# The first norm of a two-layer diffusion backbone: squares by blocks, feature sums as one-column products, and an opening order written out by hand

## Chip, cores and metric

The kernel runs on one core of one Trainium2 chip. The metric is the device time of one execution in microseconds (us). The core has five engines with a queue each: TensorE (PE in the profile; its weight loads are shown apart as PEld), VectorE (DVE), ScalarE (ACT), GpSimd (POOL) and SyncE (SP), which here issues all DMAs. An instruction waits at the head of its engine's queue until its semaphores are there, and what stands behind it on that engine waits too.

## The reference, cut to what matters

```python
def rms_norm(x, g):
    y = x * lax.rsqrt(jnp.mean(x * x, axis=-1, keepdims=True) + EPS)
    return y * g

def adaln(cond, w, b):                       # cond: c for the latent, c_ctx for the context
    return (jax.nn.silu(cond) @ w + b).reshape(cond.shape[0], N_MOD, 1, D_MODEL)

def half_ffn(h, shift, scale, gate, g, w1, w3, w2):
    n = modulate(rms_norm(h, g), shift, scale)       # n * (1 + scale) + shift
    return h + 0.5 * gate * ((jax.nn.silu(n @ w1) * (n @ w3)) @ w2)

for l in range(DEPTH):                       # 2 layers
    m, mc = adaln(c, ada_w[l], ada_b[l]), adaln(c_ctx[None], ada_w[l], ada_b[l])
    h  = half_ffn(h,  m[:, 0],  m[:, 1],  m[:, 2],  norm_g[l, 0], ...)
    hc = half_ffn(hc, mc[:, 0], mc[:, 1], mc[:, 2], norm_g[l, 0], ...)
    ...                                      # four token mixers, merge, second half FFN
```

There are 256 latent and 256 context tokens with 1024 features, all in float32. The part that matters is the very first: the norm of h over its features, the modulation 0 (shift) and 1 (scale) from a product with `ada_w`, and the first columns of `w1` and `w3`.

## The kernel before

Activations lie with features on partitions: `h` is 128 x 8 x 512, that is 8 feature blocks b of 128, and 512 columns, 256 latent and 256 context tokens. Every large product is made in three float32r products (`mm3`, lines 197 to 199): the operands are cut into a high and a low part, `hi`/`lo` for weights (`cut`, lines 182 and 183: a copy on ACT, a difference on DVE) and `nh`/`nl` for the normalised h (lines 409 and 416). A weight column is 1024 x 128, 512 KB, loaded by `raw` (line 171) into a ring of three buffers, from which `cut` makes its split; the load that is to take a buffer over waits for the DVE half of the split before it.

`start` (line 214) opens the program. It loads the small parameters, h in two halves (latent, context), the constants (`ones` and `ident`), and then, in between each other, five groups of the shift and scale columns of `ada_w` (`adaraw0` to `adaraw4`, for the feature blocks 0, 1, 2 to 3, 4 to 5, 6 to 7; 1, 1, 2, 2 and 2 MB, each with a buffer of its own) and four weight columns, called `p1_0`, `p3_0`, `p1_1`, `p3_1`. The norm squares each half of h on ACT in one instruction (line 247), sums it over the 8 blocks on DVE (`ssum`, line 248), turns that by four transposes on PE (line 368), so that a DVE reduce can sum over the 128 partitions (line 370), and then makes the reciprocal root, spreads it over 128 columns (`n_w`, line 374) and turns it back on PE (`turn`, line 379; the rstd rows).

The loop over the groups then makes the modulation of a group (32 small plain float32 products, line 257), transposes it on DVE (`adat`, line 263), normalises its blocks (`nt`, `nh`, `nl`; lines 402, 409, 416) and multiplies the blocks that are ready with the columns that are split. Each column needs 8 blocks x 3 products, so there are 96 early products. Columns for later stages (`raw20`, `raw21`, ... by the order of loading) are loaded and split in `high_priority`, which lets a scheduler move them ahead of other work on their engines. Behind the early products the program goes on with the column of `raw20`.

The lines that carry the norm:

```python
for cols in (LAT, CTX):
    q = pool.tile([128, DB, T], F32, tag="q", name=f"q{cols.start}", bufs=1)
    nc.scalar.activation(out=q, in_=self.h[:, :, cols], func=AF.Square)
    nc.vector.tensor_reduce(out=ssum[:, cols], in_=q.rearrange("p b t -> p t b"), axis=AX.X, op=ALU.add)
turn = self.rstd(ssum, 512, D, "n00")
```

Of the kernel before, what the change touches and what calls it, by code (L numbers as in the profile page):

```python
# [10 lines left out]
F32 = mybir.dt.float32  # L11
F32R = mybir.dt.float32r
AF = mybir.ActivationFunctionType
ALU = mybir.AluOpType
# [104 lines left out]
class Build:  # L119
# [94 lines left out]
    def start(self, pool):  # L214
# [3 lines left out]
        nc.sync.dma_start(out=self.small, in_=d["small"])  # L218
        for cols in (LAT, CTX):
            nc.sync.dma_start(out=self.h[:, :, cols], in_=d["h0"][:, :, cols])  # L220
        nc.sync.dma_start(out=self.const, in_=d["const"][:, 0:EARLY])
        raw, columns, banks = [], [], {}
        first = [(f"p{n}_{i}", f"ffn_w{n}", i) for i in (0, 1) for n in (1, 3)]
        groups = [range(a, b) for a, b in ((0, 1), (1, 2), (2, 4), (4, 6), (6, 8))]
        loaded = (1, 2, 3, 4, 4)
        for gi, group in enumerate(groups):
# [7 lines left out]
            with self.tc.high_priority():  # L234
                nc.sync.dma_start(out=raw[gi].rearrange("p k f -> p (k f)").rearrange("p (c f) -> p c f", f=1024),
                                  in_=d["wst"][i:i + 2 * n].rearrange("c p f -> p c f"))
            for key, name, i in first[len(columns):loaded[gi]]:
                columns.append(self.raw(self.columns(name, (0, 0), np.arange(128 * i, 128 * i + 128))))
# [5 lines left out]
        ssum = self.held("ssum")  # L244
        for cols in (LAT, CTX):
            q = pool.tile([128, DB, T], F32, tag="q", name=f"q{cols.start}", bufs=1)
            nc.scalar.activation(out=q, in_=self.h[:, :, cols], func=AF.Square)
            nc.vector.tensor_reduce(out=ssum[:, cols], in_=q.rearrange("p b t -> p t b"), axis=AX.X, op=ALU.add)
        turn = self.rstd(ssum, 512, D, "n00")
        done, ready, split = [0] * len(first), 0, 0  # L250
        for gi, group in enumerate(groups + [()]):
            n = len(group)
            if n:
                ps = self.aux(f"ada0{gi}")
                for k in range(DB):
                    for g in range(4):
                        nc.tensor.matmul(ps[32 * g:32 * g + 32, 0:64 * n], self.st[:, k, :],
                                         raw[gi][:, k, 64 * n * g:64 * n * (g + 1)], start=k == 0, stop=k == DB - 1)
                if gi == 0:
                    r = turn()  # L260
                    parts = [self.norm_parts(0, 0, s, r[:, c]) for s, c in enumerate((LAT, CTX))]
                t = self.temp(f"adat0{gi}", 64 * n)
                nc.vector.transpose(out=t, in_=ps[:, 0:64 * n])
                for m in (0, 1):
                    self.modulated(0, m, t.rearrange("p (b m r) -> p m b r", m=2, r=32)[:, m, :, 0:2],
                                   slice(group[0], group[-1] + 1))
                for b in group:
                    for part in zip(*parts):
                        for f in part:
                            f(b)  # L270
            for i in range(split):
                if i not in banks:
                    banks[i] = (self.acc, self.pair)[i % 2](first[i][0])
                for k in range(done[i], ready):
                    self.mm3(banks[i], columns[i][k], self.n(k, ALL), k == 0, k == DB - 1)
                done[i] = ready
            ready += n
            for i in range(split, loaded[gi] if n else 0):
                columns[i] = self.cut(columns[i], pool=pool, bufs=4)
            split = loaded[gi] if n else split  # L280
        self.early = {first[i][0]: banks[i] for i in banks}
        c = pool.tile([128, 2, D], F32, tag="q", name="condrow", bufs=1)
# [76 lines left out]
    def rstd(self, x, n, count, name, heads=1):  # L359
# [7 lines left out]
        for i in range(nt):  # L367
            nc.tensor.transpose(ps[:, 128 * i:128 * i + 128], x[:, 128 * i:128 * i + 128], self.cst("ident"))
        r = self.tmp.tile([128, 8], F32, tag="rs", name=f"{name}_s", bufs=2)
        nc.vector.tensor_reduce(out=r[:, 0:m], in_=ps[:, 0:n].rearrange("p (m f) -> p m f", m=m), axis=AX.X, op=ALU.add)  # L370
# [6 lines left out]
        def turn(ps=ps):  # L377
            for i in range(nt):
                nc.tensor.transpose(ps[:, 128 * i:128 * i + 128], w[:, 128 * i:128 * i + 128], self.cst("ident"))
# [257 lines left out]
    def mixing(self, l, closing):  # L637
# [5 lines left out]
        with self.tc.tile_pool(name=f"mix{l}", bufs=2) as mp:  # L643
# [5 lines left out]
            nc.sync.dma_start(out=self.late, in_=self.d["const"][:, EARLY:])  # L649
# [517 lines left out]
```

## Time and profile before

| what | value |
|---|---|
| median of 3 runs | 2267.54 us (2266.43 to 2267.88) |
| the profiled execution | 2266.95 us, span 2265.2 us |
| mean granted TensorE clock in it | 0.997 |
| PE busy | 2216.1 us, 98% of the span |
| DVE busy, ACT busy | 1479.9 us (65%), 964.6 us (43%) |
| PE busy in the first 20 us | 1.90 us |
| moved by DMA | 322.81 MB, mean 143 GB/s |

The median of the runs is the time; the profile is of one execution, whose span begins with its first and ends with its last instruction. A line of the timeline has start and length in us, engine, source line, operation, what is written from what, shapes and count; brackets hold the idle time before it and what ended it. An SPq line is a DMA's issue; the DMA view gives the time from the issue to the landing.

### The profile page before, as it was taken

To read this page: it belongs to the slowest core of one execution; us is meant where nothing else is said; L and a number is where in the kernel's file an instruction comes from. 1 tells how busy PE (TensorE), PEld (TensorE's weight loads), DVE (VectorE), ACT (ScalarE), POOL (GpSimd) and SP (SyncE) were. 2 spreads that over 40 slices of the span, in tenths; PEclk is the share of its full clock that TensorE was granted. 3 is DMA by queue.
4 is the path that set the end of the run, shared out by engine and by line. 5 is a ranking of instruction groups with operands and counts; after the bars stand their busy time and mean duration, and the time that the engine had idled before them with its cause. 6 is when DMAs were issued, how large, how long until landed. Compare 5 with 4: busy or idle time off the path is not lost.

```text
span 2265.2 us, 32288 instructions
## 1 busy us (share of the span) xinstructions
PE 2216.1 (98%) x12822; PEld 1915.5 (85%) x12822; DVE 1479.9 (65%) x2432; ACT 964.6 (43%) x1513; POOL 117.7 (5%) x124
## 2 busy tenths in 40 slices
PE   6999999999999999999999999999999999999998
PEld 4888889888888788888888898888889898998998
DVE  6788874794778645556565545665537889775554
ACT  4323223455557633342222232223224777754443
POOL 0000000000000112110000010000001000121000
PEclk9999999999999999999999999999999999999999
DMA  8566663311222232334544424454534333454553
GB/s 323 184 202 202 207 214 117 119 66 65 75 75 75 75 103 93 112 112 153 163 161 156 155 82 145 158 167 149 165 115 170 122 121 122 139 181 164 180 184 131
DMA packets 92742, 322.81 MB, mean 143 GB/s; under 512 B 9904, under 2 KB 15280, under 8 KB 91952
## 3 DMA queue, kind: packets, MB, share of 16 engines
q1 hardware_dynamic: 92592, 320.76, 42.4%
q8 instruction: 100, 1.64, 0.3%
q14 instruction: 50, 0.41, 0.1%
HBM read 315.48 MB, written 5.24 MB: 142 GB/s over the span
## 4 chain that ended last, share of the span: by engine, by line
PE 87%; DVE 9%; ACT 3%; issue 1%; DMA 0%; POOL 0%; DVEq 0%; SPq 0%; ACTq 0%; POOLq 0%
PE p L198 12%; PE p L199 12%; PE p L197 12%; PE pr L199 7%; PE pr L198 6%; PE pr L197 6%; PE g L197 3%; PE g L198 3%; PE g L199 3%; DVE cv L699 2%; DVE lo L183 2%; PE b L197 2%; PE b L198 2%; PE b L199 2%; PE ao L889 1%
## 5 line engine op out<-in xcount | busy, mean ns | idle before, releaser
L182 ACT ACTIVATE hi<-raw 128x1024 fp32r<-128x1024 f32 x430 | 454.6, 1058 | 885.7 <-issue 250.1
L183 DVE TENSOR_TENSOR lo<-raw,hi 128x1024 fp32r<-128x1024 f32 x422 | 526.2, 1248 | 293.1 <-ACT hi L182 286.9
L197 PE MATMUL p<-nh,hi 128*128 128x512 f32 (+1 forms) x1456 | 521.7, 358 | 2.4 <-ACT nh L409 1.3
L199 PE MATMUL p<-nh,lo 128*128 128x512 f32 (+1 forms) x1456 | 520.9, 358 | 2.5 <-DVE lo L183 2.5
L198 PE MATMUL p<-nl,hi 128*128 128x512 f32 (+1 forms) x1456 | 521.2, 358 | 1.2 <-DVE nl L416 1.1
L325 DVE SCALAR_TENSOR_TENSOR prods<-raw,cond 128x1024 f32<-128x1024 f32 x240 | 289.1, 1222 | 191.5 <-DMA raw<-wst 188.6
L197 PEld LDWEIGHTS p<-nh,hi 128*128 128x128 f32 x1456 | 276.6, 190 | 43.8 <-ACT nh L409 2.2
L199 PEld LDWEIGHTS p<-nh,lo 128*128 128x128 f32 x1456 | 276.6, 190 | 42.9 <-DVE lo L183 3.7
L198 PEld LDWEIGHTS p<-nl,hi 128*128 128x128 f32 x1456 | 276.6, 190 | 41.5 <-DVE nl L416 2.1
L199 PE MATMUL pr<-gh,lo 128*128 128x512 f32 (+1 forms) x656 | 231.4, 353 | 0.0
L198 PE MATMUL pr<-gl,hi 128*128 128x512 f32 (+1 forms) x656 | 229.4, 350 | 0.0
L197 PE MATMUL pr<-gh,hi 128*128 128x512 f32 (+1 forms) x656 | 228.4, 348 | 0.0
L197 PE MATMUL g<-nh,hi 128*128 128x512 f32 (+1 forms) x512 | 174.9, 342 | 0.0
L199 PE MATMUL g<-nh,lo 128*128 128x512 f32 (+1 forms) x512 | 173.4, 339 | 0.0
L198 PE MATMUL g<-nl,hi 128*128 128x512 f32 (+1 forms) x512 | 172.6, 337 | 0.0
L699 DVE SCALAR_TENSOR_TENSOR cv<-yp,cw,cv 128x512 f32<-128x512 f32 (+1 forms) x240 | 148.7, 620 | 4.8
L198 PEld LDWEIGHTS pr<-gl,hi 128*128 128x128 f32 x656 | 123.2, 188 | 19.4
L197 PEld LDWEIGHTS pr<-gh,hi 128*128 128x128 f32 x656 | 123.6, 188 | 18.0
L199 PEld LDWEIGHTS pr<-gh,lo 128*128 128x128 f32 x656 | 123.1, 188 | 17.0
L197 PEld LDWEIGHTS g<-nh,hi 128*128 128x128 f32 x512 | 97.0, 189 | 10.5 <-issue 0.6
L199 PEld LDWEIGHTS g<-nh,lo 128*128 128x128 f32 x512 | 97.0, 189 | 10.4 <-issue 0.2
L198 PEld LDWEIGHTS g<-nl,hi 128*128 128x128 f32 x512 | 97.0, 190 | 9.9 <-issue 0.2
(427 smaller groups left out, 3415.7 us busy)
## 6 DMA issues: line engine op xcount, KB each, us to landing
raw<-wst SPq DMA_DIRECT2D x556, 512.0 KB, 3.4
adaraw<-wst SPq DMA_DIRECT2D x3, 2048.0 KB, 17.1
adaraw<-wst SPq DMA_DIRECT2D x8, 512.0 KB, 7.4
cond<-cond SPq DMA_DIRECT2D x3, 1024.0 KB, 4.8
h<-h SPq DMA_DIRECT2D x2, 1024.0 KB, 7.9
adaraw<-wst SPq DMA_DIRECT2D x2, 1024.0 KB, 10.6
parked<-h SPq DMA_DIRECT2D x8, 256.0 KB, 3.9
h<-parked SPq DMA_DIRECT2D x8, 256.0 KB, 3.1
```

Source lines behind the costliest of these rows:

```text
L182: self.nc.scalar.activation(out=hv, in_=r, func=AF.Copy)
L183: getattr(self.nc, low).tensor_tensor(out=lv, in0=r, in1=hv.bitcast(F32), op=ALU.subtract)
L197: mm(out, w[0], x[0], start=start, stop=False)
L198: mm(out, w[0], x[1], start=False, stop=False)
L199: mm(out, w[1], x[0], start=False, stop=stop)
L325: nc.vector.scalar_tensor_tensor(out=products[:, s], in0=r, scalar=1.0, in1=cond[:, s], op0=ALU.mult, op1=ALU.mult, accum_out=self.mod[l][ ...
L699: nc.vector.scalar_tensor_tensor(out=o, in0=x, scalar=wk, in1=o, op0=ALU.mult, op1=ALU.add)
L889: nc.tensor.matmul(o[64 * a:64 * a + 64, 0:128], va[:, k0 + k, 64 * a:64 * a + 64], at[j, qt][a][:, 128 * k:128 * k + 128], start=k == 0, ...
```

## The change

- h is loaded in four pieces of two blocks, each for all 512 columns, instead of two halves of the tokens.
- The squares are made block by block into a ring of four buffers, even blocks on ACT, odd ones on DVE. For each block, four plain float32 products with the square as the weights and one column of `ones` as the moving operand sum over the 128 partitions: 32 products, whose results (128 x 32) one DVE reduce adds over the blocks. The constants come as an array of their own (`early`), still behind h.
- `rstd` is divided, its second half becomes `root`; an early ACT instruction (`warm`) loads the table of the root ahead of need.
- The groups 2, 3 and 4 of `ada_w` share two buffers, so that the load of group 4 waits for group 2's modulation.
- The loop over the groups is replaced by a sequence of calls, in which products of two columns stand between the modulations.

```diff
+        with self.tc.high_priority():
+            nc.sync.dma_start(out=self.small, in_=d["small"])
+            for b in range(0, DB, 2):
+                nc.sync.dma_start(out=self.h[:, b:b + 2], in_=d["h0"][:, b:b + 2])
+            nc.sync.dma_start(out=self.const, in_=d["early"])
+            load_group(0)
+            load_column()
+            load_group(1)
+            load_column()
+            load_column()
+            load_group(2)
+            load_column()
+            load_group(3)
+            load_group(4)
...
-            raw.append(pool.tile([128, DB, 256 * n], F32, name=f"adaraw{gi}"))
+            raw[gi] = pool.tile([128, DB, 256 * n], F32, tag=f"adaraw{min(gi, 2)}", name=f"adaraw{gi}",
+                                bufs=1 if gi < 2 else 2)
...
-        ssum = self.held("ssum")
-        for cols in (LAT, CTX):
-            q = pool.tile([128, DB, T], F32, tag="q", name=f"q{cols.start}", bufs=1)
-            nc.scalar.activation(out=q, in_=self.h[:, :, cols], func=AF.Square)
-            nc.vector.tensor_reduce(out=ssum[:, cols], in_=q.rearrange("p b t -> p t b"), axis=AX.X, op=ALU.add)
-        turn = self.rstd(ssum, 512, D, "n00")
+        warm = self.tmp.tile([128, 1], F32, tag="warm", name="warm", bufs=1)
+        nc.scalar.activation(out=warm, in_=self.eps, func=AF.Sqrt)
+        sums = self.aux("n00_sum")
+        for b in range(DB):
+            q = pool.tile([128, 2 * T], F32, tag="q", name=f"q{b}", bufs=4)
+            if b % 2:
+                nc.vector.tensor_tensor(out=q, in0=self.h[:, b], in1=self.h[:, b], op=ALU.mult)
+            else:
+                nc.scalar.activation(out=q, in_=self.h[:, b], func=AF.Square)
+            for i in range(4):
+                nc.tensor.matmul(sums[:, 4 * b + i:4 * b + i + 1], q[:, 128 * i:128 * i + 128],
+                                 self.cst("ones")[:, 0:1], start=True, stop=True)
+        turn = self.root(sums[:, 0:4 * DB].rearrange("p (b m) -> p m b", m=4), 512, 4, D, "n00")
...
+        ps = modulation(0)
+        r = turn()
+        parts = [self.norm_parts(0, 0, s, r[:, c]) for s, c in enumerate((LAT, CTX))]
+        modulate(0, ps)
+        normalise(0)
+        cut()
+        ps = modulation(1)
+        products(0, (0,))
+        modulate(1, ps)
+        normalise(1)
+        cut()
+        cut()
+        products(1, (0,))
+        products(0, (1,))
+        products(1, (1,))
+        ps = modulation(2)
+        products(2, (0, 1))
+        modulate(2, ps)
+        normalise(2)
+        normalise(3)
+        cut()
+        products(3, (0, 1))
+        for i in range(2):
+            products(i, (2,))
+        ps = modulation(3)
...
+        ps = modulation(4)
+        for i in range(4):
+            products(i, (4,))
...
-        c = pool.tile([128, 2, D], F32, tag="q", name="condrow", bufs=1)
+        c = pool.tile([128, 2, D], F32, tag="condrow", name="condrow", bufs=1)
...
+    def root(self, sums, n, m, count, name, ps=None):
...
         r = self.tmp.tile([128, 8], F32, tag="rs", name=f"{name}_s", bufs=2)
-        nc.vector.tensor_reduce(out=r[:, 0:m], in_=ps[:, 0:n].rearrange("p (m f) -> p m f", m=m), axis=AX.X, op=ALU.add)
+        nc.vector.tensor_reduce(out=r[:, 0:m], in_=sums, axis=AX.X, op=ALU.add)
```

On PE the four transposes of `ssum` in front become the 32 sums, and the modulation of group 0 still follows them, with `turn` behind it. The first place that differs in order is PE around the modulation of group 2 (`ada02`). `hi`/`lo` with a number are a column's split, `p1_0` and so on the products' banks. Before:

```order
L197 MATMUL p1_0_230<-nh_72,hi20_180 128x512
L198 MATMUL p1_0_230<-nl_73,hi20_180 128x512
L199 MATMUL p1_0_230<-nh_72,lo20_181 128x512
L257 MATMUL ada02_238<-adaraw2_98,st_74 32x128 x32
L197 MATMUL p1_0_230<-nh_72,hi20_180 128x512
L198 MATMUL p1_0_230<-nl_73,hi20_180 128x512
L199 MATMUL p1_0_230<-nh_72,lo20_181 128x512
L197 MATMUL p3_0_295<-nh_72,hi20_234 128x512
L198 MATMUL p3_0_295<-nl_73,hi20_234 128x512
L199 MATMUL p3_0_295<-nh_72,lo20_235 128x512
```

Now, from the sixth of the products that stand behind `ada01` on:

```order
L199 MATMUL p3_0_284<-nh_72,lo20_277 128x512
L197 MATMUL p1_0_259<-nh_72,hi20_222 128x512
L198 MATMUL p1_0_259<-nl_73,hi20_222 128x512
L199 MATMUL p1_0_259<-nh_72,lo20_223 128x512
L197 MATMUL p3_0_284<-nh_72,hi20_276 128x512
L198 MATMUL p3_0_284<-nl_73,hi20_276 128x512
L199 MATMUL p3_0_284<-nh_72,lo20_277 128x512
L278 MATMUL ada02_294<-adaraw2_102,st_74 32x128 x32
L197 MATMUL p1_1_327<-nh_72,hi20_280 128x512
```

Three products stood between `ada01` and `ada02`, now twelve, seven of them from the first use of the second column's `lo` on. Six products of `p1_1` (blocks 0 and 1) and six of `p3_1` follow, then the block 2 of the first two columns, then `ada03`.

The second place is ACT behind block 1, where `hi` is the first half of a column's split; DVE has the `lo` halves in the same order among its work for the blocks. Before:

```order
L182 ACTIVATE hi20_234<-raw5_96 128x1024
L409 ACTIVATE nh_72<-nt2_276,mod0_75 128x256
L409 ACTIVATE nh_72<-nt2_278,mod0_75 128x256
L409 ACTIVATE nh_72<-nt3_284,mod0_75 128x256
L409 ACTIVATE nh_72<-nt3_286,mod0_75 128x256
L182 ACTIVATE hi20_302<-raw10_100 128x1024
L409 ACTIVATE nh_72<-nt4_344,mod0_75 128x256
```

Now:

```order
L182 ACTIVATE hi20_276<-raw5_98 128x1024
L182 ACTIVATE hi20_280<-raw6_100 128x1024
L182 ACTIVATE hi21_570<-raw20_568 128x1024
L481 ACTIVATE nh_72<-nt2_339,mod0_75 128x256
L481 ACTIVATE nh_72<-nt2_341,mod0_75 128x256
L182 ACTIVATE hi22_601<-raw21_599 128x1024
L481 ACTIVATE nh_72<-nt3_347,mod0_75 128x256
L481 ACTIVATE nh_72<-nt3_349,mod0_75 128x256
L182 ACTIVATE hi20_355<-raw11_104 128x1024
L182 ACTIVATE hi23_637<-raw22_635 128x1024
```

The third column is now split ahead of block 2. The splits of `raw20` and `raw21`, which belong to later columns and stood behind block 5 before, now stand ahead of that of the fourth column (`raw11`).

The third place is SP, the loads behind group 1 of `ada_w`. Before:

```order
L171 DMA raw5_96<-wst 128x1024
L235 DMA adaraw2_98<-wst 128x4x1024
L171 DMA raw10_100<-wst 128x1024
L235 DMA adaraw3_102<-wst 128x4x1024
L171 DMA raw15_104<-wst 128x1024
L235 DMA adaraw4_106<-wst 128x4x1024
L171 DMA raw20_526<-wst 128x1024
```

Now:

```order
L171 DMA raw5_98<-wst 128x1024
L171 DMA raw6_100<-wst 128x1024
L232 DMA adaraw2_102<-wst 128x4x1024
L171 DMA raw11_104<-wst 128x1024
L171 DMA raw20_568<-wst 128x1024
L171 DMA raw21_599<-wst 128x1024
L232 DMA adaraw3_106<-wst 128x4x1024
L171 DMA raw22_635<-wst 128x1024
L171 DMA raw23_666<-wst 128x1024
L171 DMA raw24_719<-wst 128x1024
L232 DMA adaraw4_108<-wst 128x4x1024
```

The load of group 3 now stands behind those of `raw20` and `raw21`, which wait for the DVE halves of the second and third columns' splits; the load of group 4 stands behind `raw24`, which takes the buffer of `raw11` and waits for the DVE half of the fourth column's split. Everything on all engines behind the early products has the same order as before.

More of the change, by code (lines that the diff above doesn't have):

```diff
@@ new lines, in start, with modulation @@
+        turn = self.root(sums[:, 0:4 * DB].rearrange("p (b m) -> p m b", m=4), 512, 4, D, "n00")
+        banks, ready = {}, {}
+        def modulation(gi):
+            n = len(groups[gi])
+            ps = self.aux(f"ada0{gi}")
+            for k in range(DB):
+                for g in range(4):
+                    nc.tensor.matmul(ps[32 * g:32 * g + 32, 0:64 * n], self.st[:, k, :],
+                                     raw[gi][:, k, 64 * n * g:64 * n * (g + 1)], start=k == 0, stop=k == DB - 1)
+            return ps
@@ new lines, in modulate, with normalise @@
+        def modulate(gi, ps):
+            group, n = groups[gi], len(groups[gi])
+            t = self.temp(f"adat0{gi}", 64 * n)
+            nc.vector.transpose(out=t, in_=ps[:, 0:64 * n])
+            for m in (0, 1):
+                self.modulated(0, m, t.rearrange("p (b m r) -> p m b r", m=2, r=32)[:, m, :, 0:2],
+                               slice(group[0], group[-1] + 1))
+        def normalise(b):
+            for part in zip(*parts):
+                for f in part:
+                    f(b)
@@ L648, in mixing @@
             self.halves(list(early.values()), (512, 512, w))
-            nc.sync.dma_start(out=self.late, in_=self.d["const"][:, EARLY:])
+            nc.sync.dma_start(out=self.late, in_=self.d["late"])
             z = [self.h[:, m, cols] for m in range(DB)]
```

81 lines of the change are left out of this document (36 added, 45 removed).

## The prediction

> **What bounds the kernel now.** I read the page first, then the stretches by windows, then the chain of waits from the start, then the timeline and the DMA issues of the first 60 us.
>
> ```profile
> span 2265.2 us, 32288 instructions
> PE   2216.1 (98%) x12822; PEld 1915.5 (85%) x12822; DVE 1479.9 (65%) x2432; ACT 964.6 (43%) x1513; POOL 117.7 (5%) x124
> PE   6999999999999999999999999999999999999998
> ```
> ```profile
> 0.00:20.00 20.00, 1.90 (x28) 1.17 (x32) 8.24 (x8) 6.60 (x5) 0.20 (x4) 1.00 0.92 328
> 20.00:45.00 25.00, 23.19 (x362) 17.58 (x355) 20.71 (x52) 11.45 (x19) 0.00 (x0) 1.00 0.91 357
> 45.00:70.00 25.00, 25.00 (x111) 20.38 (x110) 14.30 (x24) 11.51 (x15) 0.00 (x0) 1.00 0.54 197
> ```
> TensorE (PE) is busy 98% of the span. The windows (length, then PE, weight loads, DVE, ACT, POOL) put 18.1 + 1.8 = 19.9 us of its idle time into the first 45 us, the only place that the change touches; behind it PE never stops, so whatever the start gains or loses reaches the end. The chain shows what it waits for:
> ```profile
> 1.18 6.43 DMA h<-h
> 7.64 1.92 ACT q L247
> 9.58 3.60 DVE ssum L248
> 13.20 1.92 ACT q L247
> 15.14 3.60 DVE ssum L248
> 18.79 0.69 PE n_ps L368 x2
> 19.48 1.87 PE ada L257 x64
> 21.35 1.06 PE n_ps L379 x4
> ```
> Square and sum of latent, then of context, one after the other: the sums leave PE at 19.48, the rstd rows at 22.41. From there the four weight columns and five modulation groups are worked off almost without a gap:
> ```profile
> 19.52 0.69 DVE L370 TENSOR_REDUCE n_s<-n_ps 128x4 f32<-128x512 f32 x1 [0.78 <-PE n_ps L368]
> ...
> 22.32 1.82 PE L257 MATMUL ada<-adaraw,st 128*32 128x64 f32 x64
> ...
> 24.85 0.19 PEld L197 LDWEIGHTS p<-nh,hi 128*128 128x128 f32 x1 [0.88 <-ACT hi L182]
> ...
> 24.96 0.19 PEld L198 LDWEIGHTS p<-nl,hi 128*128 128x128 f32 x1
> ...
> 26.54 1.95 PE L257 MATMUL ada<-adaraw,st 128*32 128x128 f32 x64
> ...
> 29.12 1.23 DVE L183 TENSOR_TENSOR lo<-raw,hi 128x1024 fp32r<-128x1024 f32 x1 [0.46 <-ACT hi L182]
> ...
> 30.27 0.31 DVE L263 STREAM_TRANSPOSE adat<-ada 128x128 f32<-128x128 f32 x1
> ...
> 35.34 1.23 DVE L183 TENSOR_TENSOR lo<-raw,hi 128x1024 fp32r<-128x1024 f32 x1 [0.46 <-ACT hi L182]
> ...
> 36.91 0.39 PE L197 MATMUL p<-nh,hi 128*128 128x512 f32 x1
> ...
> 39.25 0.40 PE L198 MATMUL p<-nl,hi 128*128 128x512 f32 x1
> ...
> 39.81 1.95 PE L257 MATMUL ada<-adaraw,st 128*32 128x128 f32 x64
> ...
> 41.69 0.51 PE L197 MATMUL p<-nh,hi 128*128 128x512 f32 x1
> ```
> Ten products lie between 36.91 and 39.25, so one takes 0.234. Behind the last modulation 60 of the 96 early products are left from 41.69 on: the four columns end at 41.69 + 60 x 0.234 = 55.7. That is the mark I compare.
>
> **The change, part by part.**
>
> *The loads.* All DMAs leave by SP and land in order:
> ```profile
> 2.56 2.07 SPq L221 DMA_DIRECT2D const<-const  x1
> 3.57 0.22 DVE L631 TENSOR_SCALAR lam<-small 128x1 f32<-128x1 f32 x2 [2.38 <-DMA small<-small]
> 26.09 0.33 SPq L171 DMA_DIRECT2D raw<-wst  x1
> 26.46 0.87 SPq L235 DMA_DIRECT2D adaraw<-wst  x1
> ```
> ```profile
> raw<-wst SPq DMA_DIRECT2D x1, 512.0 KB, 6.1
> adaraw<-wst SPq DMA_DIRECT2D x1, 2048.0 KB, 10.9
> ```
> ```profile
> raw<-wst SPq DMA_DIRECT2D x1, 512.0 KB, 3.4
> ```
> ```profile
> const<-const SPq DMA_DIRECT2D x1, 128.0 KB, 9.0
> ```
> The issue at 26.09 landed at 32.2, the next, 2 MB, at 37.4: 2.6 us a MB in 4 KB rows. A lone 512 KB takes 3.4 (third answer, the issue at 42.8). `small` is in at 3.5, so the four pieces of h are in by 3.5 + 5.2 = 8.7. But const, with the ones that the sums multiply by, is still last, where it landed at 11.6 before: now about 9.1 (at most that 11.6, if the larger rows of h gain nothing). So the squares stream, the sums don't: all start at 9.1. The squares (a quarter of 1.92 on ACT, about as much on DVE) hide under h and the sums.
>
> *The sums.* Each of the 32 products has a new 128x128 weight block and one moving column. A plain f32 product leaves two loads in the trace (32 modulation products are x64 above), so 64 loads. Two loads start 0.11 apart at 24.85 and 24.96. At the start PE runs at half speed: 64-column products took 1.82 at 22.32, 128-column ones 1.95 at 26.54 (the clock column of the windows says 1.00 there all the same; the durations decide). So 64 x 0.11 = 7.0 below, 64 x 0.22 = 14.1 above, and nothing in the rows excludes that such short products cost less (0 at best). I take half speed for the first 4.4 us, as long as the modulations ran slow from 19.48: 20 loads, then 44 x 0.11 = 4.8, together 9.2. Sums out: 9.1 + 9.2 + 0.2 = 18.5 instead of 19.5 (16.3 to 23.4).
> The Trainium skill, "TensorE: Matmul & The Clock Gate", section LDWEIGHTS, gives columns / 1.2 ns, whatever the number of moving columns: 107 ns, as the rows have it, and by it an estimate of 6.8 us for the sums. It is the rule that speaks against one-column products.
>
> *To the rstd rows.* The reduce reads 32 elements, not 512, and saves some 0.5; ada group 0 still stands between on PE. 18.5 + about 3.0 = 21.5 instead of 22.4. Gain 0.9.
>
> *Up to the second column's split* nothing differs: from 22.41 to the end of lo at 29.12 + 1.23 = 30.35 are 7.95. After: 29.45.
>
> *Group 2's modulation moves back.* Before, PE ran it at 26.54, and its transpose on DVE (30.27) follows the split at once. Now seven products that need that split stand ahead of it: 7 x 0.234 + 1.95 = 3.6, transpose at 33.1, 3.7 later against that split. The third column's split (1.15) fills a part of the gap, but does not end it. Loss 3.7.
>
> *The fourth column's split.* From the transpose at 30.27 to the end of the split at 35.34 + 1.23 = 36.57 were 6.3. Now the splits of raw20 and raw21 (columns for later) stand ahead of it on ACT and DVE: 2 x 1.15 more, end at 33.1 + 8.6 = 41.7. PE, which has products of this column (blocks 0 and 1) next, stands still for some 6 us until then.
>
> *The rest.* PE then has 28 products and group 3 (6.55 + 1.9) ahead of group 4: 50.1. On SP group 4's load is queued behind raw24, which waits for this column's buffer: issue 0.3 later, 3.4 for raw24, 5.2 for 2 MB, landing at 50.6, in place of 37.4. From there 1.9 + 48 x 0.234 = 13.1: end at 63.7. Against 55.7 that is +8.0.
>
> *The clock.*
> ```profile
> 23.90:27.30 3.40, 2.15 (x47) 1.33 (x41) 2.84 (x9) 0.97 (x2) 0.00 (x0) 1.00 1.03 408
> 976.20:979.60 3.40, 1.56 (x11) 1.36 (x12) 2.48 (x4) 0.50 (x2) 2.44 (x1) 1.00 0.87 345
> 979.60:983.00 3.40, 3.40 (x18) 3.40 (x18) 3.39 (x9) 1.85 (x5) 0.76 (x2) 0.50 0.48 159
> ```
> A stretch with PE busy 46% was followed by one at a granted clock of 0.50 (first number after POOL's); one of 63% was not. Now the stretches at 25 to 29 and 34 to 41 fall under that: each costs up to 3.4 x 0.5 = 1.7. The second is partly hidden, since group 4's load is waited for anyway. I take one: +1.7 (0 to 2.9).
> The Trainium skill, "TensorE: Matmul & The Clock Gate", Part 1, states a fixed window of about 3.4 us after which an idle array drops to half rate; by it an estimate of the same 1.7 per window, and the trace agrees in the rows above.
>
> **The sum.** -0.9 (norm), +3.7 (group 2), +2.3 (two splits), +2.9 (from the last split that PE waits for to the end, 63.7 - 41.7 = 22.0 instead of 55.7 - 36.6 = 19.1: more of PE's work is left there, and the load is late), in all +8.0; with +1.7 for the clock +9.7. The profiled execution took 2266.95, its span 2265.2 and 1.75 around it, 0.6 under the median of 2267.54 and inside the three runs. Forecast 2266.95 + 9.7 = 2276.6. The granted clock and everything behind the fourth column stay as they are; the condition row's own buffer removes a wait on q that was over long before.
>
> **Rivals.**
> 1. *The sums stay at half speed throughout* (short products may not count as work for the clock): 23.4 instead of 18.5, +4.9: 2281.5. For it: loads alone are little PE work. Against it: nothing but the modulations' 4.4 us.
> 2. *The sums are as good as free, and the change comes out even*: short products cost almost nothing, because their loads overlap. Sums out at 10.5, -8.0: +1.7, 2268.7, and even at 2267 if the clock drop fails too. Against it: the 0.11 between two loads.
> 3. *SP is not held up* (faster): were group 4's load issued back to back with the others, as at 26.46, it would land with the last of 12.4 MB (0.25 small, 2 h, 0.13 const, 8 groups, 2 columns): 12.4 x 2.6 + 2.9 before the first bytes = 35 us after the start, and the end would be 35 + 13.1 = 48.1: -7.6, 2259.3. It decides where that load lands before 55.7 - 13.1 = 42.6, so the fourth column's split must end by 33.7. Against it: that split stands behind two others and a modulation that starts at 31.
>
> **How the numbers follow.** Forecast (+4.6 to +12) 0.58; rival 1 (+12 to +16) 0.20; rival 2 (0 to +4.5) 0.12; rival 3 0.05; beyond +16, where slow sums, a late const and both clock drops come together, 0.05. 0.2% is 4.5 us, about what a measurement of this kernel can tell from no change. So slower 0.58 + 0.20 + 0.05 = 0.83, same 0.12, faster 0.05. The range leaves out rival 3, the far end and half of rival 2, 0.16 in all: 2269.5 (+2.5) to 2283.0 (+16).
>
> **What would show it.** Right: the first sum starts when const lands, near 9, and the 32 take 7 to 14 us; ada group 2 follows the second column's split; PE idles some 6 us for `hi` of the fourth column; group 4's load lands near 50; PE's idle time in the first 70 us is near 30 us instead of 20. Wrong: the sums out by 11, no PE wait over 2 us behind the rstd rows, or group 4's load in by 42.

## The result and the profile after

The change made the kernel slower: 2282.39 us (median of 4 runs, 2282.09 to 2283.16) against 2267.26 on the same chip (4 runs, 2266.43 to 2267.88), ratio 1.0067 with a 95% interval of 1.0051 to 1.0083. That is +15.1 us where +9.7 was forecast, inside the range and near its upper end. The profiled execution took 2282.57 with a span of 2280.8, 15.6 more than before.

The page and the windows over the same three stretches as before (length, then PE, weight loads, DVE, ACT, POOL, granted clock, DMA share, GB/s):

```profile
span 2280.8 us, 32418 instructions
...
PE 2233.6 (98%) x12882; PEld 1931.2 (85%) x12882; DVE 1473.9 (65%) x2434; ACT 963.2 (42%) x1516; POOL 117.4 (5%) x124
```
```profile
0.00:20.00 20.00, 10.34 (x49) 10.37 (x49) 3.35 (x9) 5.29 (x8) 0.20 (x4) 1.00 0.93 354
20.00:45.00 25.00, 19.29 (x231) 14.49 (x230) 13.31 (x32) 7.86 (x12) 0.00 (x0) 1.00 0.53 199
45.00:70.00 25.00, 22.21 (x193) 17.02 (x194) 12.81 (x31) 9.75 (x14) 0.00 (x0) 0.86 0.56 207
```

The record of the granted clock begins only at 39.7 us (at 23.9 in the kernel before), so the 1.00 up to there says nothing; the durations show half speed. By these rows PE idles 9.7 + 5.7 + 2.8 = 18.2 us in the first 70, less than the 19.9 before. But PE's busy time is 17.5 us longer, and 13.8 of that are the one-column sums. A share of busy time doesn't tell what the busy time achieves; the timeline does (start, length, engine, line, and in brackets the idle time before and what ended it). PE first:

```profile
9.66 13.79 PE L268 MATMUL n_sum<-const,q 128*128 128x1 f32 x64 [9.66 <-DMA const<-early]
...
25.24 1.12 PE L451 MATMUL n_ps<-const,n_w 128*128 128x128 f32 x4
...
33.10 0.79 PE L197 MATMUL p<-nh,hi 128*128 128x512 f32 x1 [2.23 <-ACT hi L182]
...
37.64 2.95 PE L278 MATMUL ada<-adaraw,st 128*32 128x128 f32 x64
...
47.75 0.79 PE L197 MATMUL p<-nh,hi 128*128 128x512 f32 x1 [5.56 <-ACT hi L182]
...
53.52 1.95 PE L278 MATMUL ada<-adaraw,st 128*32 128x128 f32 x64
...
59.81 1.95 PE L278 MATMUL ada<-adaraw,st 128*32 128x128 f32 x64
```

The sums start when const lands and take 13.8 us. The rstd rows are done at 25.24 + 1.12 = 26.36 instead of 22.41. Group 2's modulation runs at 37.64, not at 26.54. PE stands 5.56 us for the fourth column's `hi`, and then 12 products take the 5.8 us from 47.75 to group 3's modulation: 0.48 each instead of 0.234, nearly all of it at half clock:

```profile
46.60:53.40 6.80, 5.61 (x12) 3.64 (x12) 3.12 (x4) 2.16 (x3) 0.00 (x0) 0.50 0.73 242
```

What it waited for, on ACT, DVE and SP:

```profile
33.08 2.36 DVE L183 TENSOR_TENSOR lo<-raw,hi 128x1024 fp32r<-128x1024 f32 x2 [0.46 <-ACT hi L182]
40.67 0.32 DVE L285 STREAM_TRANSPOSE adat<-ada 128x128 f32<-128x128 f32 x1 [5.23 <-PE ada L278]
...
42.28 1.22 DVE L183 TENSOR_TENSOR lo<-raw,hi 128x1024 fp32r<-128x1024 f32 x1
...
44.21 1.22 DVE L183 TENSOR_TENSOR lo<-raw,hi 128x1024 fp32r<-128x1024 f32 x1
...
47.73 1.22 DVE L183 TENSOR_TENSOR lo<-raw,hi 128x1024 fp32r<-128x1024 f32 x1 [0.46 <-ACT hi L182]
```
```profile
38.88 1.06 ACT L182 ACTIVATE hi<-raw 128x1024 fp32r<-128x1024 f32 x1 [4.88 <-DMA raw<-wst]
```
```profile
49.41 0.71 SPq L232 DMA_DIRECT2D adaraw<-wst  x1
```

The two splits at 42.28 and 44.21 are those of `raw20` and `raw21` (ACT stood 4.88 us for the load of `raw20`, but block 2, next on ACT, came only behind the transpose at 40.67 anyway); the fourth column's is the one at 47.73, and group 4's load leaves only behind it.

As mark for the comparisons I take the start of the 96th early product, before and after:

```profile
55.62 0.39 PE L199 MATMUL p<-nh,lo 128*128 128x512 f32 x1
```
```profile
72.81 0.39 PE L199 MATMUL p<-nh,lo 128*128 128x512 f32 x1
```

The start loses 17.2 us. The span loses 1.6 less, since a half-clock stretch at 979.6 (quoted in the prediction) doesn't come in the execution after: the corresponding place lies some 17 us later and keeps its clock. In all 14 traces of this case the changes of the granted clock lie whole multiples of 3.413 us apart. Laid out from the end of the half-clock stretch at 53.39, the windows there are:

```profile
992.05:995.47 3.42, 2.15 (x14) 1.66 (x13) 2.89 (x6) 1.81 (x3) 1.83 (x1) 1.00 0.87 325
995.47:998.88 3.41, 2.58 (x22) 2.58 (x23) 2.88 (x7) 1.31 (x3) 0.63 (x2) 1.00 0.76 273
```

PE is busy 2.15 and 2.58 of 3.41 us in them, where it was 1.56 in the one at 976.2 before: the pause is now spread over two windows, and neither is followed by half clock.

### The profile page after: what moved, and what is told of

Its sections match the earlier page's. It is cut to its first block, busy times and chain, and to the rows that moved or that the text cites. A ratio compares the mean times of both kernels' runs of the same rounds, so it can differ in the third digit from the quotient of the medians.

```text
span 2280.8 us, 32418 instructions
## 1 busy us (share of the span) xinstructions
PE 2233.6 (98%) x12882; PEld 1931.2 (85%) x12882; DVE 1473.9 (65%) x2434; ACT 963.2 (42%) x1516; POOL 117.4 (5%) x124
## 4 chain that ended last, share of the span: by engine, by line
PE 87%; DVE 8%; ACT 3%; issue 1%; DMA 0%; POOL 0%; SPq 0%; DVEq 0%; ACTq 0%; POOLq 0%
PE p L197 12%; PE p L199 12%; PE p L198 12%; PE pr L199 6%; PE pr L198 6%; PE pr L197 6%; PE g L197 3%; PE g L198 3%; PE g L199 3%; DVE cv L771 2%; DVE lo L183 2%; PE b L197 2%; PE b L198 2%; PE b L199 2%; PE ao L961 1%
## 5 line engine op out<-in xcount | busy, mean ns | idle before, releaser
L199 PEld LDWEIGHTS pr<-gh,lo 128*128 128x128 f32 x656 | 123.1, 188 | 17.2
```

Of the source, the lines that this page charges most:

```text
L199: mm(out, w[1], x[0], start=False, stop=stop)
```

## The experiments

All medians, and the marks and spans of the profiled executions. "Against before" is the difference to the kernel before on the same chip (2265.95 to 2267.26). "Half clock" is the time at a granted clock of 0.50 between 100 us and 2200 us.

| kernel | median us | against before | ratio (95%) | mark | half clock | span |
|---|---|---|---|---|---|---|
| before | 2267.26 | | | 55.62 | 10.2 | 2265.2 |
| the change | 2282.39 | +15.1 | 1.0067 (1.0051 to 1.0083) | 72.81 | 6.8 | 2280.8 |
| old_norm | 2277.35 | +11.0 | 1.0047 (1.0032 to 1.0062) | 69.88 | 6.8 | 2277.9 |
| new_norm | 2270.53 | +4.2 | 1.0019 (1.0010 to 1.0029) | 60.82 | 6.8 | 2268.7 |
| warm_up | 2281.12 | +14.8 | 1.0058 (1.0041 to 1.0074) | 73.21 | 13.6 | 2283.0 |
| const_first | 2278.40 | +12.5 | 1.0050 (1.0035 to 1.0065) | 70.04 | 0 | 2274.6 |
| const_warm | 2279.91 | +14.0 | 1.0056 (1.0041 to 1.0071) | 69.31 | 6.8 | 2276.7 |
| mod2_early | 2281.68 | +15.3 | 1.0063 (1.0048 to 1.0078) | 71.42 | 10.2 | 2280.6 |
| group_loads | 2280.04 | +14.1 | 1.0062 (1.0045 to 1.0078) | 70.45 | 6.8 | 2277.0 |
| loads_mod2 | 2277.12 | +11.2 | 1.0046 (1.0031 to 1.0060) | 65.82 | 10.2 | 2275.1 |
| rows_change | 2271.41 | +4.8 | 1.0021 (1.0011 to 1.0030) | 61.00 | 6.8 | 2268.8 |
| rows_loads | 2266.90 | +0.1 | 1.0003 (0.9994 to 1.0012) | 57.69 | 6.8 | 2264.9 |
| rows_before | 2264.53 | -2.1 | 0.9990 (0.9981 to 0.9999) | 55.12 | 6.8 | 2262.9 |
| rows_group2 | 2263.99 | -2.5 | 0.9986 (0.9977 to 0.9995) | 54.93 | 6.8 | 2262.2 |

With 4 runs of a kernel the intervals reach some 3 us to either side, so medians of variants that lie closer than that don't tell them apart. There the marks are compared, and a mark is that of one execution, late loads and all.

**Which half of the change costs?** `old_norm` keeps the change's order and loads and takes back the norm, `new_norm` the other way round.

```diff
 # old_norm, against the change
-            for b in range(0, DB, 2):
-                nc.sync.dma_start(out=self.h[:, b:b + 2], in_=d["h0"][:, b:b + 2])
+            for cols in (LAT, CTX):
+                nc.sync.dma_start(out=self.h[:, :, cols], in_=d["h0"][:, :, cols])
...
-        sums = self.aux("n00_sum")
...
-        turn = self.root(sums[:, 0:4 * DB].rearrange("p (b m) -> p m b", m=4), 512, 4, D, "n00")
+        ssum = self.held("ssum")
...
+        turn = self.rstd(ssum, 512, D, "n00")
```


> The change with the first norm as before (h in halves, squares and sums over whole halves, transposes), so only the order and the loads are new. Theory A (three terms: sums 4 us late, the hand order 8, half clock 3): the sums leave PE at 19.5 as before, and what is left is the order and some of the clock: 8 to 12 us over before, 2275.5 to 2279.5, 3 to 7 under the change. Theory B (the late sums are the loss, with all that follows from starting late; the order does no harm by itself): 2267 to 2269, as before. Theory C (only the late load of group 4 counts, landing near 50 whatever the norm does): within 2 of the change, 2280 to 2284.

`new_norm` is the kernel before with the same lines exchanged the other way (and the condition row in the buffer of `adaraw0`).

> Before with the new norm alone (h in four pieces, 32 one-column sums), the loop, loads and buffers of the groups as before. Theory A: the sums leave PE near 23.5, 4 us late, and the clock comes up some 4 us later: 4 to 6 us over before, 2271 to 2273.5. Theory B: most of the 15 us, 2279 to 2283. Theory C: the load of group 4 is issued early, so it is as before, 2266 to 2269.

Measured: +11.0 for the order alone, +4.2 for the norm alone, together 15.2 against 15.1 for the change. The two parts add. The marks (14.3 and 5.2 against 17.2) add only when late loads are taken out: in the profiled execution of `old_norm`, the slowest of its four, h landed 1.5 us later than before, and const landed 1.2 us later in `new_norm` than in the change. In `new_norm` the sums took as long as in the change:

```profile
10.83 13.78 PE L254 MATMUL n_sum<-const,q 128*128 128x1 f32 x64 [10.83 <-DMA const<-const]
```

And in `old_norm` PE waits for `hi` as in the change, which puts that wait down to the order, not to the norm:

```profile
30.66 0.79 PE L197 MATMUL p<-nh,hi 128*128 128x512 f32 x1 [2.52 <-ACT hi L182]
...
45.08 0.79 PE L197 MATMUL p<-nh,hi 128*128 128x512 f32 x1 [5.71 <-ACT hi L182]
```

**Why do the sums take 13.8 us?** Either a one-column product costs 0.215 us in any case, or the clock stays at half. `warm_up` puts 22 products of 512 columns ahead of the sums; their results are not used.

```diff
+        hot = pool.tile([128, 512], mybir.dt.bfloat16, tag="hot", name="hot", bufs=1)
+        nc.vector.memset(hot, 1.0)
+        hps = self.aux("hot_ps")
+        for i in range(22):
+            nc.tensor.matmul(hps, hot[:, 0:128], hot, start=True, stop=True)
         sums = self.aux("n00_sum")
```


> The change with 22 full products on a constant tile in front of the sums, whose result is not used; they fill PE's idle time until const lands near 9.7. Theory A with its reading of the clock (one-column products don't count as work, but run at the clock they find): the first sums go at 0.11 a load instead of 0.215, after one or two stretches of 3.4 us the clock falls back, the 32 sums take 8 to 11 us instead of 13.8, and the whole is 3 to 6 us under the change: 2276 to 2279.5. If a weight load takes 0.215 whatever the clock: 13.8 us and no difference, 2281 to 2284. If one-column products do hold a clock that is up: 7 us, and 7 to 9 under the change, 2273 to 2275.5.

This one told nothing, because const came late. The extra products ended near 8.1, const landed at 11.98, and the clock had fallen just then (the granted clock is the first number after POOL's busy time):

```profile
8.10:11.60 3.50, 0.05 (x1) 0.00 (x0) 0.69 (x1) 0.63 (x1) 0.00 (x0) 0.99 1.03 369
11.60:15.00 3.40, 3.02 (x15) 3.05 (x15) 0.00 (x0) 0.63 (x1) 0.00 (x0) 0.50 1.02 418
```

So const was moved ahead of h, first alone:

```diff
+            nc.sync.dma_start(out=self.const, in_=d["early"])
             for b in range(0, DB, 2):
                 nc.sync.dma_start(out=self.h[:, b:b + 2], in_=d["h0"][:, b:b + 2])
-            nc.sync.dma_start(out=self.const, in_=d["early"])
```


> The change, with the ones and the identity loaded ahead of h, so that the sums start with h's first blocks instead of behind const. Theory A: the sums cost 64 loads of 0.215 us at half clock wherever they start, so they run from about 5.7 to 19.5 instead of 9.7 to 23.5, 4 us earlier, 2278.3. Rival: the landing of h paces them and they come out at 22 or later, 2281 to 2282.

> const_first, with 30 products of 512 columns ahead of the sums on PE (their results are not used), which run until h has landed, near 10. Theory A: the pitch of 0.215 us is the half clock, and one-column products do not keep the clock up: the sums start at 0.107 and fall back to 0.215 once a window of 3.4 us holds nothing else, out between 17 and 21, about 2277 to 2281. Rival 1: the clock stays full, 64 x 0.107 = 6.9, out at 17, 2276. Rival 2: 0.215 is the pitch of such a product at any clock, out at 24, 2283.

```profile
7.62 13.81 PE L268 MATMUL n_sum<-const,q 128*128 128x1 f32 x64 [7.62 <-ACT q L266]
```

In `const_first` the sums start at 7.62, not at 5.7, because the first piece of h landed only at 6.9 (in the change DVE had its first piece at 5.2):

```profile
6.94 0.63 ACT L266 ACTIVATE q<-h 128x512 f32<-128x512 f32 x1 [0.20 <-DMA h<-h]
```

They take the same 13.8. The mark comes 2.8 us earlier than the change's, the median is 2.6 us less above before; that late start is some 2 us of the expected 4.

`const_warm`, with the lines of `warm_up` for 30 products on top of that, decides the question. PE in the order of time (28 of the 30 are recorded), and the windows of 3.4 us from 7.6 on:

```profile
2.62 8.68 PE L264 MATMUL hot_ps<-hot 128*128 128x512 bf16 x28
11.13 10.63 PE L273 MATMUL n_sum<-const,q 128*128 128x1 f32 x64
```
```profile
7.60:11.00 3.40, 3.40 (x17) 1.55 (x16) 0.69 (x1) 0.63 (x1) 0.00 (x0) 1.00 1.01 383
11.00:14.40 3.40, 3.40 (x32) 3.37 (x31) 0.69 (x1) 1.07 (x2) 0.00 (x0) 1.00 1.01 416
14.40:17.80 3.40, 3.40 (x19) 3.40 (x18) 0.69 (x1) 0.19 (x1) 0.00 (x0) 0.51 1.04 417
17.80:21.20 3.40, 3.40 (x17) 3.40 (x18) 0.00 (x0) 0.00 (x0) 0.00 (x0) 0.50 1.02 405
```

In the window from 11.0 the profile has 32 product records, nearly all of them sums (a one-column product leaves two), at full clock, one each 0.11 us; then the granted clock halves and it has 19 and 17, one each 0.21 by the sums' length, although PE and its weight loads are busy 3.4 of 3.4 us throughout. So the pitch follows the clock (rival 2 falls), the sums don't keep the clock up (rival 1 falls), and theory A stands. The sums came out at 21.8 (they started at 11.1, 3.5 us later than in `const_first`, which ate the gain), just beyond the 21 expected. Plain float32 as such is not the reason: in the kernel before, the window from 20.47 held only modulation products of 64 columns and four transposes in that type, and behind it 128 columns took what 64 had taken (1.95 us at 26.54, 1.82 at 22.32).

```profile
20.47:23.88 3.41, 3.41 (x100) 2.91 (x92) 2.51 (x9) 1.01 (x4) 0.00 (x0) 1.00 1.03 410
```

The Trainium skill, "TensorE: Matmul & The Clock Gate", Part 1, has the clock set in a free-running window of 3.4 us by how busy PE was; the trace agrees with the window, but "busy" there is not what the profile's busy column counts.

**What of the order costs?** Three kernels, all with the new norm. `mod2_early` moves group 2's modulation ahead of the second column's products and the third column's split behind blocks 2 and 3:

```diff
         products(0, (0,))
+        ps2 = modulation(2)
         modulate(1, ps)
         normalise(1)
         cut()
-        cut()
-        products(1, (0,))
         products(0, (1,))
-        products(1, (1,))
-        ps = modulation(2)
-        products(2, (0, 1))
-        modulate(2, ps)
+        products(1, (0, 1))
+        modulate(2, ps2)
         normalise(2)
         normalise(3)
         cut()
+        products(2, (0, 1))
+        cut()
         products(3, (0, 1))
```


> The change with another order of calls alone: group 2's modulation behind the first three products, as before, and the third column's split behind block 3; the scheduler then also puts only one later column's split ahead of block 2, and group 3's and 4's loads ahead of raw21 and raw22. The norm stays. Theory A: 3.7 and about half of the rest comes back, PE's waits for hi shrink from 7.8 to under 4 us: 6 to 9 under the change, 2273 to 2276.5. Theory B: within 2 of the change, 2280 to 2284. Theory C: group 4's load lands some 8 us earlier, and the time falls by as much: 2273 to 2276, but then old_norm stays at the change's time.

It won nothing: +15.3. Group 2's modulation ran at 31.75, 6 us earlier than in the change, but the scheduler left `raw20`'s split ahead of blocks 2 and 3. ACT stood 4.56 us for that load, and PE waited 8.93 us instead of 2.23 and 5.56:

```profile
38.86 1.06 ACT L182 ACTIVATE hi<-raw 128x1024 fp32r<-128x1024 f32 x1 [4.56 <-DMA raw<-wst]
```
```profile
45.74 0.79 PE L197 MATMUL p<-nh,hi 128*128 128x512 f32 x1 [8.93 <-ACT hi L182]
```

`group_loads` takes away the other part, the later columns' loads and splits, and `loads_mod2` both:

```diff
             load_column()
-            load_group(3)
-            load_group(4)
+            with self.tc.high_priority():
+                load_group(3)
+                load_group(4)
```


> The change, but the loads of modulation groups 3 and 4 are queued ahead of raw20 and raw22 on SP, which also puts the splits of raw20 and raw21 behind the fourth column's on ACT and DVE. Theory A (each term of the order as the prediction has it): only the two splits and a little of the load go, since group 2's modulation still stands behind seven products and group 4's load still behind raw22, which waits for the fourth column's split: PE's wait for hi shrinks from 5.6 us to about 3.3, the end comes 2.5 to 3 us earlier, 2279.5. Theory B (the splits and loads of later columns are the whole 11 us of the order): 2271. Theory C (they are hidden): 2282, wait still 5.6.

> The same, and group 2's modulation moved ahead of the products of the second column, as in mod2_early. Theory A: mod2_early won nothing because raw20's split stood ahead of blocks 2 and 3 and the wait only moved; with both away the order's 11 us go nearly whole: no wait for hi over 2 us, group 4's load landing near 43 instead of 54, 2271 to 2273 (the new norm's 4 us stay). Theory B (the two parts do not interact): the gain is that of group_loads alone, 2279.5.

`group_loads`: the wait fell from 5.56 to 3.58 us and the mark by 2.4, as theory A has it (the median by about 1).

```profile
45.65 0.53 PE L197 MATMUL p<-nh,hi 128*128 128x512 f32 x1 [3.58 <-ACT hi L182]
```

`loads_mod2`: the mark fell by 7.0, far more than the 2.4 and 1.4 of the two parts by themselves (const landed 0.3, 1.1 and 1.2 us later than in the change in `group_loads`, `loads_mod2` and `mod2_early`, so that each won as much more). So they do hide each other, against theory B. But theory A promised more: 2277.12 instead of 2271 to 2273. A wait stays, for the third column's split, which now stands behind blocks 2 and 3, and group 2's modulation still ran partly at half clock (2.75 instead of 1.95):

```profile
31.87 2.75 PE L279 MATMUL ada<-adaraw,st 128*32 128x128 f32 x64
...
40.38 0.79 PE L197 MATMUL p<-nh,hi 128*128 128x512 f32 x1 [3.46 <-ACT hi L182]
```

Its mark is 10.2 behind before's, of which 5.2 are the norm (`new_norm`): 5.0 of the order's 14.3 (`old_norm`'s mark, 12.8 without its late h) remain with this variant. By the medians it is more, 11.2 - 4.2 = 7.0 of 11.0, so how much remains is known only roughly.

**Other sums.** If the fault of the sums is one column per weight load, 512 columns per load should cure it. The edit takes away more than that, also the wait for const and both rounds of transposes, and changes the products' type, so it shows that such a norm is faster and not which of these makes it so.

```diff
-            q = pool.tile([128, 2 * T], F32, tag="q", name=f"q{b}", bufs=4)
+            q = pool.tile([128, 2 * T], F32R, tag="q", name=f"q{b}", bufs=4)
...
-            for i in range(4):
-                nc.tensor.matmul(sums[:, 4 * b + i:4 * b + i + 1], q[:, 128 * i:128 * i + 128],
-                                 self.cst("ones")[:, 0:1], start=True, stop=True)
-        turn = self.root(sums[:, 0:4 * DB].rearrange("p (b m) -> p m b", m=4), 512, 4, D, "n00")
+            nc.tensor.matmul(sums, one, q, start=b == 0, stop=b == DB - 1)
+        r = self.tmp.tile([128, 512], F32, tag="rstd", name="n00_w", bufs=1)
+        nc.scalar.activation(out=r, in_=sums, func=AF.Sqrt, scale=1.0 / D, bias=self.eps)
+        nc.vector.reciprocal(out=r, in_=r)
```


> The kernel before, its order of work untouched, h in four pieces, and the sums over features as eight products of 512 columns with a 128x128 block of ones, accumulated over the blocks: every partition gets the sum, so the two rounds of transposes go, and nothing waits for const. Squares are rounded once to the products' type. Theory A (what was wrong with the change's sums is one column per weight load, not TensorE): 8 products of at most 0.43 us follow h as it lands, rstd near 12 instead of 22.4, then the loads pace it, group 4 in near 35 to 36 and the end mark near 48.5 instead of 55.7: 2259 to 2261. Rival: the first products cannot start before their own loads, so that the norm was hidden behind them, 2266.

> The change, its order of work and its queues untouched, with the same eight products for the sums. Theory A (norm and order add): sums out near 11 instead of 23.5, the waits of the order (second column's products ahead of group 2's modulation, raw20 and raw21, group 4's load) stay and keep it 8 to 11 us above the other kernel of this call, 2268 to 2271. Rival: with an earlier norm the loads pace everything, the two kernels come out within 3 us of each other, 2260 to 2263.

```profile
7.26 3.88 PE L255 MATMUL n_sum<-q,one 128*128 128x512 f32 x6 [7.26 <-ACT q L254]
11.40 1.22 PE L255 MATMUL n_sum<-q,one 128*128 128x512 f32 x2 [0.26 <-ACT q L254]
...
17.49 1.93 PE L266 MATMUL ada<-adaraw,st 128*32 128x64 f32 x64 [1.89 <-DMA adaraw<-wst]
...
25.22 3.64 PE L266 MATMUL ada<-adaraw,st 128*32 128x128 f32 x64 [3.40 <-DMA adaraw<-wst]
```
```profile
13.38 3.35 DVE L258 RECIPROCAL n_w<-n_w 128x512 f32<-128x512 f32 x1 [1.96 <-ACT n_w L257]
```

In `rows_before` the sums are out at 12.6 and the reciprocal root at 16.7, 5.7 us ahead of the rstd rows before. Yet the mark gains only 0.5: PE then waits for the modulation groups' loads, for group 2 until 25.2, does that modulation at half clock (3.64 us instead of 1.95), and from there it has the same work left as before. The rest of the median's 2.1 us lies behind the start, where this execution has one half-clock window less (6.8 us against 10.2). The expected 2259 to 2261 fell because they let the landing of group 4 set the end; it is that of group 2, behind which PE has no gap over 0.3 us. `rows_change` came out 6.9 us above it, a bit more than 2271: with the sums out of the way the order still costs, and the rival falls.

`rows_loads` is `rows_change` with a buffer for each group, groups 2, 3 and 4 loaded ahead of the fourth column, and that column's products last:

```diff
             load_column()
             load_group(2)
-            load_column()
             load_group(3)
             load_group(4)
+            load_column()
...
         products(1, (0,))
         products(0, (1,))
         products(1, (1,))
-        ps = modulation(2)
         products(2, (0, 1))
+        ps = modulation(2)
         modulate(2, ps)
         normalise(2)
         normalise(3)
-        cut()
-        products(3, (0, 1))
...
+        cut()
+        products(3, (0, 1, 2, 3, 4, 5))
         modulate(4, ps)
```


> rows_change with a buffer of its own for each modulation group, the loads of groups 2, 3 and 4 queued before the fourth column's (so no load of a later column, and no split, stands ahead of them on SP), and the fourth column's products last: blocks 0 and 1 of three columns run while group 2 loads. Theory A (what remains after the norm is the loads: in rows_before PE waited 3.4 us for group 2 at 25.2 and then never stopped): PE has done 18 products instead of 3 when group 2 comes, near 26.5, and is busy from there: 5.9 us of modulations, 78 products of 0.234 and some 1.5 of first normalisation end at 52 to 53 instead of 55.7, 2262 to 2264, 0 to 3 us under rows_before. Rival: the half clock of a PE that is busy less than half of the time before 26 eats it, 2265 to 2267.

The rival's time came: 2266.90. PE ran at half clock up to 26.6, as the rival has it, and a second stretch followed that it doesn't name. Behind group 2's modulation PE waits 2.37 us for blocks 2 and 3 with nothing left to do, and the clock halves from 33.4 to 36.8, so that products take 0.43:

```profile
33.02 0.49 PE L197 MATMUL p<-nh,hi 128*128 128x512 f32 x1 [2.37 <-ACT nh L481]
...
34.99 0.63 PE L198 MATMUL p<-nl,hi 128*128 128x512 f32 x1
35.41 0.63 PE L199 MATMUL p<-nh,lo 128*128 128x512 f32 x1
```

Last, `rows_before` with group 2's load ahead of the second column's:

```diff
-            for key, name, i in first[len(columns):loaded[gi]]:
+            for key, name, i in first[len(columns):(1, 1, 3, 4, 4)[gi]]:
```


> rows_before, with the load of modulation group 2 (2 MB) queued ahead of the second column's (0.5 MB) instead of behind it; nothing else is moved but some loads and splits behind the fourth column. Theory A (in rows_before the landing of group 2 is the last wait, 3.4 us at 25.2, and PE never stops behind it): group 2 comes 1.3 us earlier, PE's wait shrinks to about 2.1, the last of the four columns' 96 products starts near 53.8 instead of 55.1, 2263.0 to 2263.8. Rival 1: the second column, now landing near 25, is what the splits wait for, and nothing is won, 2264 to 2265. Rival 2: an earlier group 2 shifts the half-clock stretch, not the work, and the gain doubles, 2262.

```profile
21.76 2.99 PE L266 MATMUL ada<-adaraw,st 128*32 128x128 f32 x64 [0.72 <-DMA adaraw<-wst]
...
29.85 2.81 PE L266 MATMUL ada<-adaraw,st 128*32 128x128 f32 x64 [2.79 <-DMA adaraw<-wst]
```

The wait for group 2 shrank from 3.40 to 0.72, but PE now waits 2.79 for group 3: the wait moved on by one load, and the mark gained 0.2. At 2263.99 it is faster than the kernel before, and so than the change, though its mark is only 0.7 us earlier than before's; from `rows_before` its interval doesn't tell it.

## Why the prediction was right, and where its sizes failed

The sign and the order's mechanism held; the norm's term came out with the other sign. The terms, each as the difference of the same two rows before and after:

| step | forecast | measured | rows after |
|---|---|---|---|
| norm to the rstd rows | -0.9 | +4.0 | 26.36 against 22.41 |
| to the second column's split | 0 | 0 | end 33.08 + 1.18 = 34.26 against 30.35 |
| group 2 behind seven products | +3.7 | +6.5 | transpose 40.67 against 30.27 |
| two splits ahead of the fourth column's | +2.3 | +2.0 | end 48.95 against 36.57 |
| from there to the mark | +2.9 | +4.8 | 72.81 against 55.62 |
| clock, as a term of its own | +1.7 | inside group 2's row and the mark's | |
| behind the start | 0 | -1.6 | the window at 979.6 |

The step that failed is the norm's: "I take half speed for the first 4.4 us". It was the half speed of the whole 13.8 us that came, which is rival 1, and its reason is the one given there in brackets: such products do not count for the clock, as `const_warm` shows. Its price, +4.9 over the forecast, is the step from -0.9 to +4.0. The measured +15.1 thus lies in rival 1's band (+12 to +16, chance 0.20) and not in the forecast's own (+4.6 to +12), and rival 1's 2281.5 is nearer to 2282.39 than the forecast's 2276.6: the range held because it took that rival in. There is luck in it too. At the mark the loss was 17.2, beyond the range; the 1.6 that bring it back are a half-clock window far behind the start, a term that the prediction put at nothing ("everything behind the fourth column stay as they are"). Its "behind it PE never stops" isn't so either: of the 49 us that PE idles before, only 19.9 lie in the first 45.

The order's terms had the right places. What they lack is the clock. Of group 2's 2.8 us too little, 7 products at 0.43 instead of 0.234 make 1.4 and the modulation at 2.95 instead of 1.95 makes 1.0. In the last term, 12 products at 0.48 make 12 x 0.25 = 3.0, more than the 1.9 that were missing. Group 4's load left at 49.41 and landed 8.8 later, near 58.2; PE reached its modulation at 59.81, 1.6 behind it. At full clock, by an estimate from these rows, PE would have been there 3.0 earlier and would have waited for the load, so 1.6 of the 3.0 count and the rest is hidden behind the load, as the prediction has it; the load itself, 9.3 behind the split's end instead of 8.9, is the remainder. Together the clock cost some 1.4 + 1.0 + 1.6 = 4.0 us where 1.7 was taken (0 to 2.9): PE ran at half clock in both stretches that were named (up to 39.7, without having been at full clock before, and from 46.6 to 53.4), and only a part of the second was hidden.

Of the signs named beforehand, the first sum at 9.7, group 2's place and the wait of 5.6 us came. The sign of PE's idle time failed: it fell to 18.2 us instead of rising to 30, since the profile counts the sums as busy, which the prediction overlooked; with the sums counted as idle it is 18.2 + 13.8 = 32.0. Group 4's load came near 58.2 instead of 50.6, because the split that it waits for ended at 48.95 instead of 41.7.

Rival 3 would have needed the fourth column's split before 33.7; it ended at 48.95. `loads_mod2` frees SP of the later loads and still doesn't reach the kernel before.

What isn't settled: how much of the order's remainder in `loads_mod2` is the third column's wait and how much is half clock; no run takes the two apart.

## What to carry to other kernels

Price an instruction stream on PE at the clock that it itself earns: here products of one column per weight load never brought the clock up in 13.8 us, and a clock that was up fell after one window of them, however busy PE looked. When a wait is taken away, look up which wait stands directly behind it: `mod2_early`, `rows_before` and `rows_group2` each removed a wait, and the next load or split took over most of it (`group_loads` kept its 2.4 us). Work moved ahead of a step that others wait for, here seven products ahead of a modulation and two splits ahead of a third, costs its own length and then the clock that falls in the gap.

## What the runs showed of the hardware

- Loads of a 128x128 f32 block with one column each kept PE busy 3.40 of 3.40 us (`const_warm`), and the granted clock fell from 1.00 to 0.50 all the same.
- The half clock comes in whole windows of 3.41 us (1, 2, 3 or 5 of them in these traces). Its time behind the start differs among the profiled executions: none in `const_first`, 13.6 us in `warm_up`. Take the span, less the mark, less half of the half-clock time behind it, and all 14 kernels give 2203.0 to 2204.6 us: the rest of the program is constant to 1.6 us, and 1.7 us a window come on top. Executions of one kernel differ in the same way: in the runs of the kernel before that go with `rows_loads`, 2263.72 us has a mean granted clock of 0.998 and 2268.43 us one of 0.995. So whether an early change moves these windows or they fall by chance isn't shown.
- The landing of const, issued in the same place, varied from 9.66 (the change) to 11.98 us (`warm_up`); the first half of h was in at 7.64 before and at 9.16 in `old_norm`.
- DVE's reciprocal of 128x512 took 3.35 us, where a copy of that size took 0.43 in the change.
